# Modulation rows: from TensorE matmuls per block to VectorE products and one sum per row

## The chip, the cores and the metric

The program runs on one core of one Trainium2 chip. The metric is the device time of one execution in microseconds (us). Five engines run in parallel, each its own instructions in order: TensorE (PE), VectorE (DVE), ScalarE (ACT), GpSimd (POOL) and SyncE (SP), which here only issues DMAs. In the trace PEld is TensorE's weight load.

## The reference

Two models of two layers run one behind the other. The first (`first_block`, kernel layers F0 and F1) has a mixer of four branches and a SwiGLU feed-forward on 256 tokens of 1024 features. The second (`second_block`, kernel layers S0 and S1) takes its result `x` and a context `ctx` of another 256 tokens; its mixer has a gated branch, an attention and a convolution of 31 taps, and its feed-forward a convolution of 3 taps. Each layer of the second is modulated:

```python
cmod = adaln(c_ctx, w_mod[l], b_mod[l], 2 if last else 6)
sh1, sc1, g1, sh2, sc2, g2 = [m[:, None, :] for m in adaln(c, w_mod[l], b_mod[l], 6)]
hl = modulate(rms_norm_2(x_lat, norm1_g[l]), sh1, sc1)
...
x_lat = x_lat + g1 * mixer_merge(pa, o, pc, P, lam_init)
h2 = modulate(rms_norm_2(x_lat, norm2_g[l]), sh2, sc2)
x_lat = x_lat + g2 * conv_ffn(h2, P)
```

`adaln` is a product of the activated vector `c` (1024) with `w_mod[l]` (1024 x 6144) plus a bias. The kernel treats it as six rows for each of the two layers, twelve in all: row r of layer l is 1024 results, from a 1024 x 1024 part of `w_mod`. There are two vectors, one for `x` and one for the context; the last layer needs the context's rows 0 and 1 only.

## The kernel before

All matrix products go through split numbers: a weight unit of 128x1024 float32 (512 KB) is loaded by SP into `raw` (6 buffers), rounded to `hi` on ScalarE (L275), and the rest `lo = raw - hi` is formed on VectorE (L278); `hi` and `lo` have 4 buffers each. A product is then three matmuls, hi x hi, hi x lo and lo x hi (L509 to L511). Units are numbered through the kernel (`lo_405` is the split of unit 405), and all of F0, F1, S0, S1 read this one stream. F0 lies at about 0 to 600 us of the trace, F1 at 600 to 1255, S0 at 1260 to 1800, S1 from there to the end.

Beside the stream run "side lanes", work without matrix weights that is interleaved with the feed-forward of another layer. Beside F1's feed-forward (1012 to 1183 us) it is the context's mixer of S0, with the convolution's taps on VectorE (L1478, tile `cv`) and GpSimd (L1482). S0's feed-forward begins near 1447 us; its unit evaluates the short convolution and the gate on VectorE (L1526 to L1530, tiles `gh`, `th`), and `hl` is the split of its result.

The modulation rows are a generator (`mods`, L1116) that is advanced by `fill` from the gate and feed-forward loops of F0, F1 and S0. Each row has 8 blocks of 128x1024 (`wm`, 4 buffers, loaded by SP, L1137). A block costs four matmuls of 128x32 by 128x256 in full float32 (L1151, tile `am`), which sum over the 8 blocks in PSUM; the trace shows two records for each of these matmuls. Two blocks are done in a step (`MSTEP`). At the end of a row come a copy (`mo`, ScalarE), two transposes (L1161), the bias (L1164), and for rows 2 and 5 a DMA. In the layer's feed-forward of 512 tokens three steps follow each unit (`FF`).

The order of the instructions on each engine is not the order of the source: a scheduler that works with a timeline of its own moves the generator's instructions forward where it takes them to be ready.

## Time and profile before

| | us |
|---|---|
| median of three runs | 2175.38 (2171.88 to 2175.63) |
| the profiled execution | 2178.79 |
| its span, first to last instruction | 2176.7 |
| TensorE busy in it | 2109.6 (97%) |
| VectorE busy in it | 1413.5 (65%) |
| ScalarE busy in it | 1073.1 (49%) |
| GpSimd busy in it | 286.6 (13%) |

The profile is of one execution, with times from the span's start. The busy share says how much of the span an engine worked; the chain of work that ended last is followed back from the last instruction, and says which engine's work set the end, stage by stage. The mean granted clock of TensorE was 0.986 of full speed.

### The profile page before, as it was taken

How to read it: one execution, taken by the hardware profiler on the slowest of the kernel's cores; microseconds unless marked ns; L12 is line 12 of the kernel's file. 1: busy time of each engine (PE TensorE's matmuls, PEld its weight loads, DVE VectorE, ACT ScalarE, POOL GpSimd, SP SyncE). 2: the span in 40 equal slices, each digit the busy share in tenths (PEclk: the TensorE clock that was granted, in tenths of full speed). 3: DMA queues.
4: the chain of work that ended last, by engine and by line, in shares of the span. 5: the costliest groups of instructions: out<-in, count | busy, mean ns of one | idle time of the engine just before them, and what ended most of it. 6: DMA issues, size and time to landing. Idle time of an engine off the chain costs nothing.

```text
span 2176.7 us, 34980 instructions
## 1 busy us (share of the span) xinstructions
PE 2109.6 (97%) x13600; PEld 1818.3 (84%) x13600; DVE 1413.5 (65%) x2567; ACT 1073.1 (49%) x1900; POOL 286.6 (13%) x268
## 2 busy tenths in 40 slices
PE   8999999999999999999999997999999999899999
PEld 6788899889887888999889876687787888678997
DVE  7756656755579466668966479774435546976774
ACT  5555544634455556457554464653313335465552
POOL 2101112100032011121200035100000002610000
PEclk9999999999999999999999998899999999999999
DMA  9545655667765454556556654245535233224553
GB/s 334 162 139 175 204 188 191 228 151 260 240 185 178 134 161 145 159 181 223 194 115 203 212 206 145 95 145 186 197 112 192 88 90 114 88 87 141 185 189 116
DMA packets 102357, 366.71 MB, mean 168 GB/s; under 512 B 12560, under 2 KB 12720, under 8 KB 102192
## 3 DMA queue, kind: packets, MB, share of 16 engines
q1 hardware_dynamic: 99920, 358.65, 50.8%
q0 software_dynamic: 2272, 5.83, 1.0%
q8 instruction: 107, 1.75, 0.3%
q14 instruction: 58, 0.48, 0.1%
HBM read 361.76 MB, written 2.68 MB: 167 GB/s over the span
## 4 chain that ended last, share of the span: by engine, by line
PE 89%; DVE 6%; issue 2%; ACT 1%; DMA 1%; SPq 0%; POOL 0%; POOLq 0%; DVEq 0%; ACTq 0%
PE mm L509 26%; PE mm L510 26%; PE mm L511 26%; DVE cv L1478 2%; PE am L1151 2%; PE ax L1286 1%; DVE lo L278 1%; PE ax L936 1%; PE ax L1316 1%; ACT hi L275 1%; PE ay L591 1%; PE ay L462 1%; PE ax L891 1%; PE ax L889 1%; PE ax L1306 0%
## 5 line engine op out<-in xcount | busy, mean ns | idle before, releaser
L278 DVE TENSOR_TENSOR lo<-raw,hi 128x1024 fp32r<-128x1024 f32 (+2 forms) x552 | 697.0, 1265 | 527.8 <-ACT hi L275 494.0
L275 ACT ACTIVATE hi<-raw 128x1024 fp32r<-128x1024 f32 (+1 forms) x564 | 593.8, 1054 | 809.5 <-PE mm L510 384.6
L509 PE MATMUL mm<-hThi,hi 128*128 128x256 f32 (+1 forms) x2408 | 725.5, 303 | 6.7 <-DVE gu L1265 2.1
L510 PE MATMUL mm<-hTlo,hi 128*128 128x256 f32 (+1 forms) x2408 | 721.4, 300 | 4.8 <-issue 4.2
L511 PE MATMUL mm<-hThi,lo 128*128 128x256 f32 (+1 forms) x2408 | 719.3, 300 | 4.1 <-issue 3.5
L509 PEld LDWEIGHTS mm<-hThi,hi 128*128 128x128 f32 x2408 | 462.1, 193 | 45.4 <-issue 16.4
L510 PEld LDWEIGHTS mm<-hTlo,hi 128*128 128x128 f32 x2408 | 464.1, 193 | 21.6 <-issue 8.0
L511 PEld LDWEIGHTS mm<-hThi,lo 128*128 128x128 f32 x2408 | 462.9, 193 | 17.4 <-issue 2.8
L510 PE MATMUL mm<-lo,hThi 128*128 128x512 f32 (+2 forms) x480 | 183.5, 383 | 6.6 <-DVE lo L278 6.6
L509 PE MATMUL mm<-hi,hThi 128*128 128x512 f32 (+2 forms) x480 | 183.4, 388 | 5.2 <-DVE rb L580 3.1
L511 PE MATMUL mm<-hi,hTlo 128*128 128x512 f32 (+2 forms) x480 | 181.8, 381 | 0.5 <-DVE hTlo L472 0.5
L509 PE MATMUL mm<-hi,hh 128*128 128x512 f32 x440 | 171.5, 390 | 0.0
L510 PE MATMUL mm<-lo,hh 128*128 128x512 f32 x440 | 171.3, 389 | 0.0
L511 PE MATMUL mm<-hi,hl 128*128 128x512 f32 x440 | 170.9, 389 | 0.0
L509 PEld LDWEIGHTS mm<-hi,hThi 128*128 128x128 f32 x480 | 91.4, 191 | 26.6 <-issue 7.1
L510 PEld LDWEIGHTS mm<-lo,hThi 128*128 128x128 f32 x480 | 91.5, 191 | 26.3 <-DVE lo L278 8.4
L511 PEld LDWEIGHTS mm<-hi,hTlo 128*128 128x128 f32 x480 | 91.2, 190 | 17.3 <-issue 0.8
L509 PEld LDWEIGHTS mm<-hi,hh 128*128 128x128 f32 x440 | 82.6, 188 | 18.0 <-ACT hi L275 0.8
L511 PEld LDWEIGHTS mm<-hi,hl 128*128 128x128 f32 x440 | 82.6, 188 | 17.3
L510 PEld LDWEIGHTS mm<-lo,hh 128*128 128x128 f32 x440 | 82.6, 188 | 16.9
L1478 DVE SCALAR_TENSOR_TENSOR cv<-yp,kept,cv 128x256 f32<-128x256 f32 x120 | 86.1, 720 | 2.5 <-ACT cv L1474 0.7
L511 PE MATMUL mm<-yh,lo 128*128 128x256 f32 x256 | 72.8, 285 | 0.0
(348 smaller groups left out, 2757.4 us busy)
## 6 DMA issues: line engine op xcount, KB each, us to landing
raw<-in_w_f SPq DMA_DIRECT2D x364, 512.0 KB, 3.9
raw<-in_w_s SPq DMA_DIRECT2D x190, 512.0 KB, 3.5
wm<-in_w_mod SPq DMA_DIRECT2D x96, 512.0 KB, 5.1
bc<-csd POOLq DMA_DIRECT2D x32, 128.0 KB, 5.6
mrow<-md SPq DMA_DIRECT2D x6, 512.0 KB, 5.6
row<-in_rows SPq DMA_DIRECT2D x4, 512.0 KB, 5.8
raw<-in_w_f SPq DMA_DIRECT2D x4, 510.0 KB, 5.0
par<-in_par_s SPq DMA_DIRECT2D x2, 918.5 KB, 4.7
```

The source lines that it names most:

```text
L275: nc.scalar.activation(hi[:, :n], raw[:, :n], AF.Copy)
L278: ins = eng.tensor_sub(lo[:, :n], raw[:, :n], hi[:, :n].bitcast(F32)).ins
L462: nc.tensor.transpose(pss[k // 2][:, o:o + 128], xs[k // 4][:, 128 * (k % 4):128 * (k % 4) + 128], self.ident)
L509: nc.tensor.matmul(ps, ah, bh, start=first, stop=False)
L510: nc.tensor.matmul(ps, ah, bl, start=False, stop=False)
L511: nc.tensor.matmul(ps, al, bh, start=False, stop=last)
L591: nc.tensor.transpose(ps[:, b * 256 + t * 128:b * 256 + t * 128 + 128], nat[t][:, (b0 + b) * 128:(b0 + b) * 128 + 128], self.ident)
L889: nc.tensor.matmul(pair[j][:, 0:128], q[j][:, :128], k[j][:, :128], start=True, stop=True)
L891: nc.tensor.matmul(pair[j][:, 128:384], q[j][:, 128:], k[j], start=True, stop=True)
L936: nc.tensor.matmul(ps[64 * j:64 * j + 64, 0:256], vv, pt[:, 0:256], start=True, stop=False, skip_group_check=True)
L1151: nc.tensor.matmul(ps[32 * j:32 * j + 32, :256], self.ctp[:, 32 * kk:32 * kk + 32], loaded[i - k + kk][:, 256 * j:256 * j + 256], start=kk ...
L1478: nc.vector.scalar_tensor_tensor(c, y[:, j:j + 256], wj, c, op0=ALU.mult, op1=ALU.add)
```

## The change

Rows 0 and 1 of layer 0 stay as they are, but with one block in a step. For the ten other rows each block is multiplied on VectorE by its scalar per partition (`ct`, one column for each of the 8 blocks and the two vectors) and added up in SBUF: tile `macc`, 128x1024 float32, one for each vector, two instructions of 128x512 for each (L1169 of the new source for block 0, a plain product; L1171 for blocks 1 to 7, product and sum). After block 7 a matmul with a matrix of ones in one column (`onep`) sums over the partitions: 4 matmuls for each vector (L1177). In rows 2 to 5 of layer 1 only one vector is needed. The blocks have 2 buffers in place of 4, and `macc` has 2. The feed-forward of F0 and F1 advances the generator after three of four units, that of S0 by 2 steps for the first 64 and by 3 after that.

```diff
--- before.py
+++ after.py
@@ -27,7 +27,7 @@
 UNIT = 1024
 GROUP = {n: g for g, ns in (("a", "sm p pt dp at on yo osq"), ("c", "cth cv lj cn"), ("p", "tap"), ("g", "gz gsq gu ga"), ("m", "mo"))
          for n in ns.split()}
-KEEP = 1154 + 4 + 2 * (280 + 80 + 96 + 48)
+KEEP = 1154 + 4 + 64 + 2 * (280 + 80 + 96 + 48)
 LIM = 2.4e19
 OVER = 2.0 ** 118
 
@@ -310,7 +310,6 @@
     POOL_TAPS = 20
     HP = 300
     HELD = 3
-    FF = 3
     LOP = 4
     AHP = 0
     PACE = False
@@ -319,8 +318,8 @@
     FRONT = 7
     GHP = (300, 0)
     SIDE2 = 5
-    MSTEP = 2
-    WM = 4
+    MSTEP = 1
+    WM = 2
     HL = 4
     AHEAD = 4
     RA = 3
@@ -822,8 +821,10 @@
             fn(m, pg, pu, hi[:, o], lo[:, o])
             hid.append((hi[:, o], lo[:, o]))
             self.run_side(side)
-            if ntok == 512 or self.filled < 48:
-                self.fill(self.FF if ntok == 512 else 1)
+            if ntok == 512:
+                self.fill(2 if self.filled < 64 else 3)
+            elif i % 4 < 3 and self.filled < 48:
+                self.fill(1)
         return hid
 
     def swiglu_unit(self, m, pg, pu, hi, lo):
@@ -1123,6 +1124,10 @@
             nc.vector.scalar_tensor_tensor(th, th, 1.0, raw, op0=ALU.add, op1=ALU.mult)
             nc.vector.tensor_scalar(self.ct, th, 0.5, None, op0=ALU.mult)
             nc.gpsimd.memset(self.ctp, 0.0)
+            self.onep = self.keep(64)
+            nc.gpsimd.memset(self.onep, 0.0)
+            nc.gpsimd.memset(self.onep.rearrange("p (w m) -> p w m", m=32)[:, 0, 0:1], 1.0)
+            nc.gpsimd.memset(self.onep.rearrange("p (w m) -> p w m", m=32)[:, 1, 1:2], 1.0)
             nc.vector.tensor_copy(self.ctp.rearrange("p (k m) -> p k m", k=8)[:, :, 0:2], self.ct.rearrange("p (k w) -> p k w", k=8))
         bm = self.keep(48)
         nc.sync.dma_start(bm, dr["b_mod"][l])
@@ -1141,16 +1146,37 @@
             nw = 2 if l == 0 or r < 2 else 1
             while len(loaded) <= min(47, i + self.MSTEP):
                 load()
-            if k == 0:
+            early = l == 0 and r < 2
+            if k == 0 and early:
                 ps = self.ax_ps("am")
-            if (k + 1) % self.MSTEP:
-                yield
-                continue
-            for kk in range(k + 1 - self.MSTEP, k + 1):
-                for j in range(4):
-                    nc.tensor.matmul(ps[32 * j:32 * j + 32, :256], self.ctp[:, 32 * kk:32 * kk + 32],
-                                     loaded[i - k + kk][:, 256 * j:256 * j + 256], start=kk == 0, stop=kk == 7,
-                                     skip_group_check=True, tile_position=(0, 32 * j))
+            if early:
+                if (k + 1) % self.MSTEP:
+                    yield
+                    continue
+                for kk in range(k + 1 - self.MSTEP, k + 1):
+                    for j in range(4):
+                        nc.tensor.matmul(ps[32 * j:32 * j + 32, :256], self.ctp[:, 32 * kk:32 * kk + 32],
+                                         loaded[i - k + kk][:, 256 * j:256 * j + 256], start=kk == 0, stop=kk == 7,
+                                         skip_group_check=True, tile_position=(0, 32 * j))
+            else:
+                if k == 0:
+                    sums = [self.wp.tile([128, UNIT], F32, tag="macc", name=f"macc{l}_{r}_{w}", bufs=2) for w in range(nw)]
+                for h in range(2):
+                    o = slice(512 * h, 512 * h + 512)
+                    for w in range(nw):
+                        c = self.ct[:, 2 * k + w:2 * k + w + 1]
+                        if k == 0:
+                            nc.vector.tensor_scalar(sums[w][:, o], loaded[i][:, o], c, None, op0=ALU.mult)
+                        else:
+                            nc.vector.scalar_tensor_tensor(sums[w][:, o], loaded[i][:, o], c, sums[w][:, o],
+                                                           op0=ALU.mult, op1=ALU.add)
+                if k == 7:
+                    ps = self.ax_ps("am")
+                    for w in range(nw):
+                        for j in range(4):
+                            nc.tensor.matmul(ps[32 * j:32 * j + 32, :256], self.onep[:, 32 * w:32 * w + 32],
+                                             sums[w][:, 256 * j:256 * j + 256], start=w == 0, stop=w == nw - 1,
+                                             skip_group_check=True, tile_position=(0, 32 * j))
             if k < 7:
                 yield
                 continue
```

Three places show how the instructions lie now. `lo_n` is unit n's split, `macc{l}_{r}_{w}` the sum of row r of layer l for vector w, `wm{l}_{r}_{k}` block k. The first is VectorE in F1's feed-forward (about 1015 us), before:

```order
L1220 TENSOR_TENSOR kept_77<-kept_77 128x64
L1225 TENSOR_TENSOR kept_77<-kept_77 128x2x16 x2
L278 TENSOR_TENSOR lo_296_11123<-raw_296_11047,hi_296_11122 128x1024
L278 TENSOR_TENSOR lo_297_11160<-raw_297_11065,hi_297_11159 128x1024
L1461 SCALAR_TENSOR_TENSOR yp_1137_11150<-cth_1138_11151,mm_1135_11088 128x256
L278 TENSOR_TENSOR lo_298_11191<-raw_298_11089,hi_298_11190 128x1024
L278 TENSOR_TENSOR lo_299_11229<-raw_299_11120,hi_299_11228 128x1024
L1461 SCALAR_TENSOR_TENSOR yp_1142_11218<-cth_1143_11219,mm_1140_11156 128x256
L1478 SCALAR_TENSOR_TENSOR cv_1139_11155<-yp_1137_11150,kept_77,cv_1139_11155 128x256 x3
```

and now:

```order
L278 TENSOR_TENSOR lo_296_11115<-raw_296_11039,hi_296_11114 128x1024
L1251 TENSOR_TENSOR kept_77<-kept_77 128x2x16
L1171 SCALAR_TENSOR_TENSOR macc0_4_0_6246<-wm0_4_2_11570,kept_77,macc0_4_0_6246 128x512
L1171 SCALAR_TENSOR_TENSOR macc0_4_1_6247<-wm0_4_2_11570,kept_77,macc0_4_1_6247 128x512
L1487 SCALAR_TENSOR_TENSOR yp_1136_11142<-cth_1137_11143,mm_1134_11080 128x256
L278 TENSOR_TENSOR lo_297_11152<-raw_297_11057,hi_297_11151 128x1024
L1171 SCALAR_TENSOR_TENSOR macc0_4_0_6246<-wm0_4_2_11570,kept_77,macc0_4_0_6246 128x512
L1171 SCALAR_TENSOR_TENSOR macc0_4_1_6247<-wm0_4_2_11570,kept_77,macc0_4_1_6247 128x512
```

Between the splits of units 296 and 297 and behind 297 stand products of row 4 of layer 0, and no longer only the splits and the side work.

The second is TensorE in S0's feed-forward (about 1475 us), before, behind the matmuls of unit 409, with the semaphores that an instruction waits for:

```order
L510 MATMUL mm_1733_15905<-hTlo_1655_15227,hi_409_15815 128x512
L511 MATMUL mm_1733_15905<-hThi_1654_15226,lo_409_15816 128x512
L1151 MATMUL am_1731_15903<-wm1_1_1_15885,kept_77 32x256 x2
L1151 MATMUL am_1731_15903<-wm1_1_2_15901,kept_77 32x256 [waits DMAHW1_49]
L1151 MATMUL am_1731_15903<-wm1_1_2_15901,kept_77 32x256 x3
L1151 MATMUL am_1731_15903<-wm1_1_3_15976,kept_77 32x256 [waits DMAHW4_49]
L1151 MATMUL am_1731_15903<-wm1_1_3_15976,kept_77 32x256 x3
L509 MATMUL mm_1738_16000<-hThi_1648_15220,hi_410_15845 128x512 [waits Activation_49]
```

and now, behind those of unit 408:

```order
L509 MATMUL mm_1728_15925<-hTlo_1655_15270,hi_408_15789 128x512
L510 MATMUL mm_1728_15925<-hThi_1654_15269,lo_408_15790 128x512
L1177 MATMUL am_1732_16009<-macc1_0_0_15762,kept_77 32x256 [waits DVE_49]
L1177 MATMUL am_1732_16009<-macc1_0_0_15762,kept_77 32x256
L508 MATMUL mm_1729_15926<-hThi_1648_15263,hi_409_15845 128x512 [waits Activation_49]
L509 MATMUL mm_1729_15926<-hTlo_1649_15264,hi_409_15845 128x512
L510 MATMUL mm_1729_15926<-hThi_1648_15263,lo_409_15846 128x512
```

The blocks' matmuls, which waited for DMAs, are gone, and the first sum of row 0 of layer 1 stands there and waits for VectorE.

The third is VectorE at the end of that row, before, around the split of unit 411:

```order
L1527 SCALAR_TENSOR_TENSOR gh_1727_15873<-mm_1725_15811,kept_77,gh_1727_15873 128x2x255
L1529 SCALAR_TENSOR_TENSOR th_1728_15874<-th_1728_15874,gh_1727_15873 128x512
L1530 TENSOR_TENSOR th_1728_15874<-th_1728_15874,mm_1726_15812 128x512
L278 TENSOR_TENSOR lo_411_15909<-raw_411_15747,hi_411_15908 128x1024
L840 TENSOR_TENSOR hl_1724_15810<-th_1728_15874,hh_1723_15809 128x512
L278 TENSOR_TENSOR lo_412_15939<-raw_412_15813,hi_412_15938 128x1024
L1526 SCALAR_TENSOR_TENSOR gh_1734_15966<-mm_1732_15904,kept_77,gh_1734_15966 128x2x255
```

and now:

```order
L1555 SCALAR_TENSOR_TENSOR th_1721_15818<-th_1721_15818,gh_1720_15817 128x512
L1171 SCALAR_TENSOR_TENSOR macc1_0_0_15762<-wm1_0_6_15919,kept_77,macc1_0_0_15762 128x512
L1552 SCALAR_TENSOR_TENSOR gh_1726_15903<-mm_1724_15841,kept_77,gh_1726_15903 128x2x255
L1171 SCALAR_TENSOR_TENSOR macc1_0_1_15763<-wm1_0_6_15919,kept_77,macc1_0_1_15763 128x512
L1171 SCALAR_TENSOR_TENSOR macc1_0_0_15762<-wm1_0_7_15997,kept_77,macc1_0_0_15762 128x512
L1171 SCALAR_TENSOR_TENSOR macc1_0_1_15763<-wm1_0_7_15997,kept_77,macc1_0_1_15763 128x512
L278 TENSOR_TENSOR lo_411_15930<-raw_411_15787,hi_411_15929 128x1024
L1556 TENSOR_TENSOR th_1721_15818<-th_1721_15818,mm_1719_15774 128x512
L1171 SCALAR_TENSOR_TENSOR macc1_0_0_15762<-wm1_0_7_15997,kept_77,macc1_0_0_15762 128x512
```

Products of blocks 6 and 7 stand among the instructions of the gate, and two of the gate's (L1556 and L1553) stand behind the split of unit 411.

## Rows read from the trace of the kernel before

**Rows 1.** Page, busy time of each engine; then the chain that ended last, by engine.

```profile
PE 2109.6 (97%) x13600; PEld 1818.3 (84%) x13600; DVE 1413.5 (65%) x2567; ACT 1073.1 (49%) x1900; POOL 286.6 (13%) x268
PE 89%; DVE 6%; issue 2%; ACT 1%; DMA 1%; SPq 0%; POOL 0%; POOLq 0%; DVEq 0%; ACTq 0%
```

**Rows 2.** Busy time of each engine in three stretches; window, its length, busy per engine (instructions).

```profile
core 0: us, PE busy (x) PEld busy (x) DVE busy (x) ACT busy (x) POOL busy (x), PEclk, DMA share, GB/s
420.00:558.00 138.00, 133.24 (x1127) 127.67 (x1126) 77.01 (x111) 59.10 (x88) 3.47 (x3) 0.96 0.69 209
1012.00:1154.00 142.00, 133.14 (x1058) 123.67 (x1058) 110.93 (x238) 80.64 (x187) 27.21 (x31) 0.96 0.59 181
1447.00:1471.00 24.00, 24.00 (x131) 19.94 (x130) 19.12 (x45) 11.80 (x16) 0.00 (x0) 1.00 0.46 154
```

**Rows 3.** Pieces of the chain, in order of time: start, us, what (x records).

```profile
406.24 0.56 PE am L1151 x6
556.12 1.00 PE am L1151 x16
...
1270.07 4.55 DMA wm<-in_w_mod
...
1456.73 0.99 PE am L1151 x12
1479.69 1.42 PE am L1151 x20
...
1517.97 1.00 PE am L1151 x16
1530.12 1.86 PE am L1151 x32
...
1692.32 1.86 PE am L1151 x32
```

**Rows 4.** The chain by line, in 1012 to 1154, 1260 to 1320, 1447 to 1525.

```profile
by line: PE mm L509 21.4%; PE mm L510 20.7%; PE mm L511 20.5%; DVE cv L1478 7.5%; issue 5.8%; DVE lo L278 5.0%; PE ax L1286 4.5%; PE ax L1316 3.5%; ACT hi L275 1.4%; PE am L1151 1.4%; PE ax L1306 1.2%; DVE rc L1297 0.9%; DVE mx L1292 0.8%;
by line: PE mm L510 20.3%; PE mm L509 18.8%; PE mm L511 18.5%; DVE cv L1478 11.9%; DMA wm<-in_w_mod 7.6%; DVE lo L278 6.7%; issue 5.1%; PE am L1151 4.8%; DVE rb L580 2.3%; DVE ss L1242 2.0%; DVE ss L415 1.2%; DVE ra L569 1.1%; DVEq L278 0.0
by line: PE mm L509 31.2%; PE mm L510 30.4%; PE mm L511 29.8%; PE am L1151 8.2%; PE am L1161 0.6%
```

**Rows 5.** Timeline of VectorE, single rows: start, us, line, operation, out<-in, shapes.

```profile
1034.40 0.94 DVE L1478 SCALAR_TENSOR_TENSOR cv<-yp,kept,cv 128x256 f32<-128x256 f32 x1
1035.27 0.41 DVE L1265 SCALAR_TENSOR_TENSOR gz<-gsq,mm 128x256 f32<-128x256 f32 x1
...
1446.38 1.21 DVE L278 TENSOR_TENSOR lo<-raw,hi 128x1024 fp32r<-128x1024 f32 x1
...
1451.44 0.74 DVE L1526 SCALAR_TENSOR_TENSOR gh<-mm,kept,gh 128x510 f32<-128x510 f32 x1
1452.10 1.22 DVE L278 TENSOR_TENSOR lo<-raw,hi 128x1024 fp32r<-128x1024 f32 x1
...
1469.72 1.22 DVE L278 TENSOR_TENSOR lo<-raw,hi 128x1024 fp32r<-128x1024 f32 x1 [0.18 <-ACT hi L275]
```

**Rows 6.** Instructions of one line on VectorE: duration in ns, min/median/max.

```profile
L618 DVE SCALAR_TENSOR_TENSOR x<-yg,rs,x x3: 745/751/1783, 1259.5 to 1260.9; 128x512 f32<-128x512 f32 x3
...
L1478 DVE SCALAR_TENSOR_TENSOR cv<-yp,kept,cv x120: 461/485/2630, 1025.6 to 1897.9; 128x256 f32<-128x256 f32 x120
```

**Rows 7.** Timeline of TensorE, two rows; in brackets the idle time before, and its releaser.

```profile
1274.66 0.64 PE L1151 MATMUL am<-wm,kept 128*32 128x256 f32 x8 [1.43 <-DMA wm<-in_w_mod]
...
1474.09 0.39 PE L509 MATMUL mm<-hThi,hi 128*128 128x512 f32 x1
```

**Rows 8.** DMA issues of the modulation blocks: KB each, median us to landing.

```profile
wm<-in_w_mod SPq DMA_DIRECT2D x96, 512.0 KB, 5.1
```

**Rows 9.** Timeline of GpSimd, the taps of the convolution, 20 in a row.

```profile
1028.10 20.09 POOL L1482 TENSOR_TENSOR cv<-cv,tap 128x256 f32<-128x256 f32 x20 [10.93 <-ACT tap L1481]
```

**Rows 10.** Groups by line, VectorE: busy us, mean ns of one, then idle before.

```profile
L1478 DVE SCALAR_TENSOR_TENSOR cv<-yp,kept,cv 128x256 f32<-128x256 f32 x120 | 86.1, 720 | 2.5 <-ACT cv L1474 0.7
```

## The prediction

> **What bounds the kernel now.** I read the page's busy times and its chain first. TensorE is busy in 97% of the span and VectorE in 65%; 89% of the chain that ended last is TensorE's own work and 6% VectorE's [rows 1]. So an instruction taken from TensorE shortens the kernel, and one given to VectorE is free, only where VectorE has room. An average does not say where that is, so I went to the stages, and in each asked for three things: the chain's share of the modulation matmuls, the busy time of VectorE, and what ends TensorE's waits.
>
> There are four stages. In F0's feed-forward (420 to 558 us) VectorE works 77.0 of 138 us [rows 2], and all eight modulation bursts from 406 to 556 us are pieces of the chain [rows 3]: room, and something to win. In F1's feed-forward (1012 to 1154 us), where the context stream's convolution taps run as side work, VectorE works 110.9 of 142 us [rows 2], and the chain runs through VectorE's taps for 7.5% and its splits for 5.0%, through the modulation matmuls for 1.4% [rows 4]: hardly any room, and hardly anything to win. At the start of S0 (1260 to 1320 us) the chain has 4.8% of modulation matmuls and 7.6% of waiting for a modulation block, but 11.9% of VectorE's taps behind them [rows 4]. In S0's feed-forward (1447 us on) the chain is TensorE alone [rows 4], with 17 bursts in it between 1456 and 1692 us [rows 3].
>
> **What goes.** Ten of twelve rows leave TensorE: 80 of 96 blocks with 4 matmuls each, 320 of 384. What returns is one sum per row: 6 rows of 8 matmuls and 4 rows of 4, 64. The net is 256 fewer. A burst of 8 matmuls (two records each, x16) holds the chain for 1.00 us, one of 16 for 1.86 us [rows 3], so about 0.12 us for one. All 256 are worth at most 256 x 0.12 = 31 us, if nothing takes their place.
>
> **What comes.** 256 VectorE instructions of 128x512: 224 multiply-adds and 32 plain products. The nearest row is the kernel's own multiply-add of that size with a scalar per partition, in the feed-forward convolution: 0.74 us, and the next instruction begins 0.66 us after it began (1451.44 to 1452.10) [rows 5]. That one reads PSUM and SBUF. The one with both tensors in SBUF, as here, has 751 ns as its median, but 1783 ns at worst [rows 6]. I take a pitch of 0.67 us for each, from the median; the upper end comes with the rivals. Sum: 256 x 0.67 = 172 us of VectorE, on top of 1413.5. It must be hidden entirely, and the new order does not spread it evenly: 60 of the instructions stand in each of F0's and F1's feed-forward stretches, and all 128 of layer 1 in S0's.
>
> **F0.** 60 x 0.67 = 40 us more on 77.0 makes 117 of 138 us. It fits. Eight bursts go, the first of 0.56 and seven of 1.00 us (the last of them stands in [rows 3]), 7.6 us; two row sums of 1.00 come back. **-5.6 us.**
>
> **F1.** 60 x 0.67 = 40 more on 110.9 makes 151 in a stretch of 142 us. VectorE would be over by 9 us, if all of its own work stayed in it and none of its waits closed up. The new order puts 28 of these instructions between the splits lo_296 and lo_304, ahead of the taps that stood there (shown above). The splits are produced several units ahead of their use, so part of the 9 us is absorbed. Ends: -2.0 (1.4% of 142, nothing lost) and +9. I take the half nearer to the full stretch, **+4 us**.
>
> **Start of S0.** The modulation matmuls and the wait for their block (4.55 us in the chain [rows 3], 1.43 of TensorE's own idle time [rows 7]) leave this place, as layer 1's first product is now placed at lo_405. 12.4% of 60 is 7.4 us; but behind them VectorE's taps are in the chain, and they will be late next. Between 0 and -7.4 I take **-4 us**.
>
> **S0's feed-forward, the first row.** Here a new wait arises. The sum of row 0 stands on TensorE right behind the matmuls with lo_408, and its operand is finished on VectorE just before lo_411 (both shown above). TensorE executes in order, so the whole stream waits behind it. When is VectorE there? Before, lo_405 starts at 1446.4 and lo_411 at 1469.7 [rows 5]; between them VectorE has about 18.5 us of work (19.1 in 1447 to 1471, less lo_411's part [rows 2]), of which two instructions of the gate, 2 x 0.67, now stand later. 27 new instructions stand between: 27 x 0.67 = 18. So VectorE is there at 1446.4 + 17 + 18 = 1481.5. TensorE is there at 1474.1, where it begins with unit 409 before [rows 7], less one burst of 1.0: 1473.1. **The stall is 8 us.** Ends: 5, if more of VectorE's work is put off, and 12, if each new product waits for its block besides (below). Up to 1518 us six bursts go, one of 1.42 and five of 1.00 (0.99 the first) [rows 3], 6.4 us; one sum of 1.0 comes. Together +8 + 1.0 - 6.4 = **+2.6 us**.
>
> **S0's feed-forward, the rest.** Now VectorE is a row ahead of its reader: the sum of row 2 stands behind unit 423 on TensorE, its operand is ready before lo_424, and a split is made more than two units before its use (lo_411 at 1469.7 [rows 5], when TensorE has yet to begin with unit 409 [rows 7]). Eleven bursts go, from 1530 to 1692 us: 1.86 for the first and the last [rows 3]; with the nine between, 224 records in all at 1.00/16, 14.0 us. One sum of 8 matmuls and four of 4 come back, 3.0. **-11.0 us.**
>
> **The loads.** Count, size and queue of the 96 loads stay. But the blocks have two buffers in place of four, and a buffer is now released by VectorE. In row 0 of layer 1 four multiply-adds, some three instructions of the gate of like size and every other time a split (1.22 us [rows 5]) lie between a release and the need of the block that takes its place: 7 x 0.67 = 4.7, or 5.9 us; a block takes 5.1 us from issue to landing [rows 8]. I price it at nothing, since VectorE's own lateness covers the difference, and keep the other end as a rival. Behind a waiting load SP holds back the loads of weights, whose six buffers cover tens of us in S0.
>
> **Sum.** -5.6 + 4 - 4 + 2.6 - 11.0 = -14.0 us, against the profiled execution of 2178.8: 2164.8. That execution lies 3.4 above the median of the three runs, so against 2175.4 the forecast is **2161 us**.
>
> **Rival A: all is hidden.** VectorE runs far enough ahead that no sum waits. F0 -5.6, F1 -2.0, start -7.4, S0 -6.4 + 1.0 - 11.0 = -16.4: -31.4, and 2144 us against the median. For it: VectorE's 65%. Against it: the 142-us stretch, and the place of row 0's sum.
>
> **Rival B: the two buffers.** If the load is 1 us late for each block after the first two of rows 0 and 1 of layer 1, VectorE, which is the later engine there, is held 14 x 1 = 14 us, and TensorE with it: -14.0 + 14, that is 2175 us, no change. For it: TensorE already waited 1.43 us for a block with four buffers [rows 7]. Against it: 4.7 to 5.9 us against 5.1 leaves as much room for no wait at all.
>
> **Rival C, the slower side: the products in F1 cost more than their median.** GpSimd's taps run beside them: 20 from 1028 to 1048 us [rows 9]. In the same microseconds VectorE's tap multiply-add with both tensors in SBUF takes 0.94 us [rows 5], where its median is 485 ns [rows 6], while the multiply-add beside it that reads PSUM takes 0.41 [rows 5]. Over the kernel the taps have a mean of 720 ns [rows 10], 1.48 times the median. By that factor each of the 60 products of F1 costs 0.35 us more: +21 us, in the one stretch where VectorE is full. The sum becomes -14.0 + 21 = +7, 2182 us. It decides from 14/60 = 0.23 us per product on; below that the kernel is still faster. Against it: GpSimd's 20 taps last 20.09 us [rows 9] of the stretch's 142, and the taps on VectorE, which pay the same now, are only put off.
>
> The Trainium skill speaks against this change here (page "SBUF — State Buffer", section "Who interferes with whom"): a VectorE instruction with two SBUF inputs contends with a GpSimd instruction that reads SBUF, and whichever comes second is blocked until the other ends; one with a single SBUF input is not. The trace agrees: 0.94 and 0.41 us side by side [rows 5]. By that rule VectorE can be held no longer than GpSimd itself is busy, 20 us at most in this stretch, of which the taps of now pay a part already; rival C's 21 us would then be its upper end, and not its middle.
>
> **How the numbers follow.** Forecast 0.46; A 0.15; B 0.17; C 0.22. The kernel is called changed beyond 0.2%, 4.4 us, about what a measurement can tell. Faster: all of the forecast and A, and a bit of B: 0.64. Same: most of B and the lower end of C: 0.13. Slower: the rest, 0.23. The range has to reach A's lower end (start and F0 a little better than priced) and C's: 2139 to 2186. The forecast's own range is 2150 to 2170.
>
> **What will show it.** Right: TensorE idle for some 8 us about 1475 us, ended by VectorE's line of the products; no gain in F1; from 1530 us on the stream of matmuls unbroken but for row sums. The products' median near 0.74 us, with a mean above it in F1 alone. Rival A: that idle time is absent and S0's start is early by over 5 us. Rival B: VectorE idle before products, ended by the DMA of a block, some 14 times about 1 us. Rival C: F1's stretch longer than 142 us by over 15 us, with products of 1 us and more beside GpSimd's taps. I am wrong altogether if VectorE's lateness reaches PSUM: if TensorE waits for gate results in every unit of S0's feed-forward, not once.

## The result, and the profile after

| | before | changed |
|---|---|---|
| median, us (six runs each) | 2175.83 (2171.88 to 2180.49) | 2153.59 (2149.02 to 2158.38) |
| ratio | | 0.989 (95%: 0.9868 to 0.9912) |
| profiled execution, us | 2178.79 | 2158.38 |
| its span, us | 2176.7 | 2156.2 |

The changed kernel is faster by 22.2 us; 14.0 were forecast. The direction and the range held, the size was 8 us short. Below it turns out that the 14 had several errors in it which partly cancelled, and that both kernels carry a cost of 14 to 16 us that the prediction never named.

The first view is the page of the changed kernel: busy time of each engine, then the chain that ended last by engine, then by line. The code's lines have shifted: products are L1169 (first block) and L1171, row sums L1177, the matmuls per block that are left L1158, the weight stream L508 to L510.

```profile
PE 2071.8 (96%) x13088; PEld 1801.9 (84%) x13088; DVE 1557.3 (72%) x2823; ACT 1070.1 (50%) x1900; POOL 293.8 (14%) x271
PE 84%; DVE 9%; DMA 3%; issue 2%; ACT 1%; POOL 0%; SPq 0%; POOLq 0%; DVEq 0%; ACTq 0%
PE mm L508 25%; PE mm L510 25%; PE mm L509 25%; DMA wm<-in_w_mod 2%; DVE cv L1504 2%; DVE lo L278 2%; DVE macc L1171 2%; PE ax L1312 1%; PE ax L937 1%; PE ax L1342 1%; ACT hi L275 1%; PE am L1158 1%; PE ay L461 1%; PE ay L590 1%; PE ax L892 1%
```

Against [rows 1]: TensorE has lost 512 records, two for each of the 256 net matmuls, and 37.8 us of busy time; VectorE has gained 143.8 us. TensorE's share of the chain falls from 89 to 84%, and the loads of modulation blocks (`wm<-in_w_mod`) and the products now hold 2% each (to one more digit 2.5% and 1.8%, 54 and 39 us). The gain of about 38 us on TensorE has thus been paid back in part through VectorE and through DMAs.

The next view answers [rows 2], the same three stretches with the busy time of each engine.

```profile
core 0: us, PE busy (x) PEld busy (x) DVE busy (x) ACT busy (x) POOL busy (x), PEclk, DMA share, GB/s
420.00:558.00 138.00, 133.46 (x1049) 128.34 (x1049) 112.17 (x173) 60.31 (x92) 4.93 (x5) 0.98 0.79 239
1012.00:1154.00 142.00, 129.27 (x1043) 122.73 (x1043) 137.49 (x259) 75.11 (x163) 28.53 (x26) 0.95 0.64 206
1447.00:1471.00 24.00, 17.52 (x77) 12.70 (x76) 23.36 (x36) 9.08 (x13) 0.00 (x0) 0.86 0.56 169
```

VectorE in F0's feed-forward is at 112 of 138 us (117 expected), and in F1's at 137.5 of 142. In the third stretch TensorE has lost 6.48 us, and that is one single wait, on TensorE's timeline (start, duration, instruction, idle time before it and what ended it):

```profile
1451.53 0.39 PE L510 MATMUL mm<-hThi,lo 128*128 128x512 f32 x1
1458.40 1.07 PE L1177 MATMUL am<-macc,kept 128*32 128x256 f32 x4 [6.48 <-DVE macc L1171]
1459.40 0.80 PE L508 MATMUL mm<-hThi,hi 128*128 128x512 f32 x1
```

This is the stall that was forecast at 8 us: the sum of layer 1's row 0, at its place behind the matmuls of unit 408, waiting for VectorE.

**Where the time went, stage by stage.** Both kernels read the same numbered weight units, so the start of the first matmul that reads unit n (the trace's matmuls, numbered by the program's order) is a clock that both share. The table has that time in the changed kernel minus that time in the one before, as the difference over each stage (negative is a gain). The last column is the same for a second pair of kernels, e2 and e1 below, in which one disturbance is out of the way; it is given here so that the table stands once.

| stage (units) | forecast | changed - before | e1 - e2 |
|---|---|---|---|
| start and F0's mixer (to 114) | 0 | -5.8 | -6.1 |
| F0's feed-forward (114 to 162) | -5.6 | -5.9 | -4.1 |
| F1's mixer (162 to 294) | 0 | -1.7 | -3.0 |
| F1's feed-forward (294 to 366) | +4.0 | -1.3 | +7.2 |
| start and mixer of S0 (366 to 408) | -4.0 | -7.6 | -2.6 |
| S0's feed-forward, first six units (408 to 414) | +2.6 to unit 416, then -11.0 | +6.8 | +6.8 |
| S0's feed-forward, the rest (414 to 456) | | -2.8 | -13.7 |
| after that (456 to 558) | 0 | -2.2 | -1.6 |
| sum | -14.0 | -20.5 | -17.1 |

-20.5 is also the difference of the two spans. How well does this clock repeat? Between e1 and e9, two executions of one kernel on two chips, it differs by 1.1 us up to unit 12, by 1.5 us in F1's mixer, and by at most 0.6 us in every other stage.

Four stages differ much from the forecast: the start, F1's feed-forward, S0's start, and S0's feed-forward behind its first row. The waits of VectorE say where to look. The view is that of the tile `macc` in the changed kernel: durations of the products in ns (min/median/max), then VectorE's idle time ahead of them (us, times).

```profile
L1171 DVE SCALAR_TENSOR_TENSOR macc<-wm,kept,macc x224: 727/745/1225, 413.3 to 1612.1; 128x512 f32<-128x512 f32 x112
...
  DMA wm<-in_w_mod: 32.2, 14
```

VectorE waited 14 times for a block, 32.2 us in all. The number of times is rival B's, but the size is not uniform. Two of the waits hold 20.8 us, as VectorE's timeline shows (the last row ahead of each wait, and the wait):

```profile
482.78 0.42 DVE L841 TENSOR_TENSOR hl<-tt,hh 128x256 fp32r<-128x256 f32 x1
493.41 1.42 DVE L1171 SCALAR_TENSOR_TENSOR macc<-wm,kept,macc 128x512 f32<-128x512 f32 x2 [10.21 <-DMA wm<-in_w_mod]
...
1557.51 1.42 DVE L1171 SCALAR_TENSOR_TENSOR macc<-wm,kept,macc 128x512 f32<-128x512 f32 x2 [1.35 <-DMA wm<-in_w_mod]
1569.53 1.41 DVE L1171 SCALAR_TENSOR_TENSOR macc<-wm,kept,macc 128x512 f32<-128x512 f32 x2 [10.61 <-DMA wm<-in_w_mod]
```

A block takes 4.4 us from issue to landing at the median of this kernel (5.1 before, [rows 8]); here one is in the chain with 18.15 us from 475.16 and one with 13.26 us from 1556.18. What the DMAs did at the first place, in windows of 10 us of the changed kernel (the last two columns are the DMA share and GB/s):

```profile
480.00:490.00 10.00, 10.00 (x85) 10.00 (x84) 3.20 (x6) 3.91 (x6) 0.00 (x0) 1.00 0.54 37
490.00:500.00 10.00, 5.46 (x31) 5.26 (x30) 6.59 (x10) 2.69 (x4) 0.00 (x0) 0.67 0.91 341
```

For 10 us the DMA engines are busy in 54% of the time and move 37 GB/s; then they move 341. TensorE runs on its reserve of splits and stands idle for 4.5 us after 490. The mean granted clock of that window is 0.67, and of 495 to 500 us it is 0.50, the lower of its two levels (1.2 of 2.4 GHz), so the idle time is followed by slow matmuls. The chain has one of the same shape ahead of the hole and one behind it:

```profile
467.87 0.12 PE mm L510
...
497.03 0.21 PE mm L510
```

What was issued just ahead of each hole is on GpSimd's timeline:

```profile
469.85 1.81 POOL L1195 DMA_DIRECT2D md<-kept  x2 [35.73 <-DVE kept L1190]
...
1553.41 0.96 POOL L1195 DMA_DIRECT2D md<-kept  x1 [136.85 <-DVE kept L1190]
```

These are the stores of the gate rows 2 and 5, which are in both kernels: 1024 floats of one vector go from `col` (128 partitions x 8) to DRAM in a transposed order, so that by the access pattern no two neighbours of a partition lie side by side in DRAM and each run is a single float of 4 bytes. (The trace does not show these runs: it records such a store as 16 packets of 256 bytes for each vector.) The kernel before has the same hole behind the same store (issued at 460.24 and at 1122.99), in its own windows:

```profile
465.00:480.00 15.00, 10.24 (x85) 8.96 (x84) 4.29 (x7) 4.03 (x6) 0.00 (x0) 0.85 0.46 26
1125.00:1145.00 20.00, 15.77 (x119) 15.35 (x119) 6.85 (x10) 6.34 (x12) 0.00 (x0) 0.91 0.53 28
```

In its chain they are two pieces called "issue", of 3.54 us at 473.75 and 4.23 us at 1137.70, which I had read past. That these stores cause the holes was a theory at this point; the first pair of experiments is on it.

### The profile page after: what moved, and what is told of

It reads as the page before. It is cut to its first block, busy times and chain, and to the rows that moved or that the text cites. A ratio compares the mean times of both kernels' runs of the same rounds, so it can differ in the third digit from the quotient of the medians.

```text
span 2156.2 us, 34229 instructions
## 1 busy us (share of the span) xinstructions
PE 2071.8 (96%) x13088; PEld 1801.9 (84%) x13088; DVE 1557.3 (72%) x2823; ACT 1070.1 (50%) x1900; POOL 293.8 (14%) x271
## 4 chain that ended last, share of the span: by engine, by line
PE 84%; DVE 9%; DMA 3%; issue 2%; ACT 1%; POOL 0%; SPq 0%; POOLq 0%; DVEq 0%; ACTq 0%
PE mm L508 25%; PE mm L510 25%; PE mm L509 25%; DMA wm<-in_w_mod 2%; DVE cv L1504 2%; DVE lo L278 2%; DVE macc L1171 2%; PE ax L1312 1%; PE ax L937 1%; PE ax L1342 1%; ACT hi L275 1%; PE am L1158 1%; PE ay L461 1%; PE ay L590 1%; PE ax L892 1%
## 5 line engine op out<-in xcount | busy, mean ns | idle before, releaser
L508 PE MATMUL mm<-hThi,hi 128*128 128x256 f32 (+1 forms) x2408 | 723.1, 302 | 14.6 <-DVE gz L1291 12.1
L510 PE MATMUL mm<-hThi,lo 128*128 128x256 f32 (+1 forms) x2408 | 717.2, 299 | 4.6 <-DVE lo L278 4.5
L508 PEld LDWEIGHTS mm<-hThi,hi 128*128 128x128 f32 x2408 | 460.2, 192 | 44.6 <-issue 13.6
L510 PEld LDWEIGHTS mm<-hThi,lo 128*128 128x128 f32 x2408 | 461.0, 192 | 24.2 <-DVE lo L278 5.0
L508 PE MATMUL mm<-hi,hThi 128*128 128x512 f32 (+2 forms) x480 | 181.7, 386 | 5.2 <-DVE rb L579 3.1
L1171 DVE SCALAR_TENSOR_TENSOR macc<-wm,kept,macc 128x512 f32<-128x512 f32 x224 | 161.8, 763 | 31.5 <-DMA wm<-in_w_mod 31.3
L510 PE MATMUL mm<-hi,hTlo 128*128 128x512 f32 (+2 forms) x480 | 180.2, 378 | 0.0
L508 PE MATMUL mm<-hi,hh 128*128 128x512 f32 x440 | 173.1, 394 | 4.2 <-DVE xn L1564 4.2
L510 PE MATMUL mm<-hi,hl 128*128 128x512 f32 x440 | 172.6, 393 | 0.0
L509 PEld LDWEIGHTS mm<-lo,hThi 128*128 128x128 f32 x480 | 90.9, 190 | 28.3 <-DVE lo L278 12.4
L508 PEld LDWEIGHTS mm<-hi,hThi 128*128 128x128 f32 x480 | 90.9, 190 | 26.4 <-issue 6.9
L510 PEld LDWEIGHTS mm<-hi,hTlo 128*128 128x128 f32 x480 | 90.5, 189 | 16.3 <-issue 0.3
L508 PEld LDWEIGHTS mm<-hi,hh 128*128 128x128 f32 x440 | 83.6, 190 | 22.4 <-issue 5.0
L510 PEld LDWEIGHTS mm<-hi,hl 128*128 128x128 f32 x440 | 83.7, 190 | 17.7
```

The source lines that it names most:

```text
L508: nc.tensor.matmul(ps, ah, bh, start=first, stop=False)
L509: nc.tensor.matmul(ps, ah, bl, start=False, stop=False)
L510: nc.tensor.matmul(ps, al, bh, start=False, stop=last)
L1171: nc.vector.scalar_tensor_tensor(sums[w][:, o], loaded[i][:, o], c, sums[w][:, o], op0=ALU.mult, op1=ALU.add)
```

## The experiments

**The gate rows stored in runs (e1, e2).** The same edit in both kernels: `col` is transposed on TensorE, copied by ScalarE, and stored as 8 runs of 512 bytes per vector. Nothing else changes.

```diff
-            for which in range(nw):
-                if r in (2, 5):
-                    nc.gpsimd.dma_start(md[which, r // 3, :].rearrange("(j p) -> p j", p=128), col[:, which, :])
+            if r in (2, 5):
+                ps = self.ax_ps("am")
+                nc.tensor.transpose(ps[:8 * nw, :128], col[:, :nw, :].rearrange("p w m -> p (w m)"), self.ident)
+                mr = self.tmp("mo", 256)
+                nc.scalar.activation(mr[:8 * nw, :128], ps[:8 * nw, :128], AF.Copy)
+                for which in range(nw):
+                    nc.gpsimd.dma_start(md[which, r // 3, :].rearrange("(j p) -> j p", p=128), mr[8 * which:8 * which + 8, :128])
```

The changed kernel with it:

> Edit: in the changed kernel the gate rows (r = 2 and 5) go to DRAM as 8 runs of 512 bytes per vector (one transpose on TensorE and one copy on ScalarE more per row) and not as 1024 single floats; results are the same. Theory 1: the single-float stores leave the DMA queues almost empty-handed for 10 to 15 us (trace of the changed kernel: 39 GB/s at 485 to 490 us, 29 GB/s at 1560 to 1565 us), and VectorE, which executes in order, stands behind a product that waits for its block (10.2 us at 493 us, 10.6 us at 1569 us). Then the time falls by 8 to 16 us against the changed kernel, to 2138 to 2146 us, and VectorE's idle time before products that wait for a block falls from 32 us to under 12. Theory 2: VectorE is simply full in these stretches and the store only coincides: within 3 us of 2154.

Measured: 2139.64 us (2132.13 to 2142.38), 0.9826 of before (0.9799 to 0.9853). The kernel before with it:

> Edit: the same store by runs of 512 bytes in the kernel before. Theory 1 (the single-float store starves the weight loads): TensorE's unexplained gaps of 3.5 us at 474 us and 4.2 us at 1138 us go, and the time falls by 6 to 10 us, to 2166 to 2170 us; less than in the changed kernel, where VectorE stands behind two buffers. Theory 2: the gaps have another cause, and the time stays within 3 us of 2176.

Measured: 2159.20 us (2156.87 to 2165.57), 0.9926 of before (0.9901 to 0.9952): 16.4 us less, where I expected 6 to 10. So six stores of 4 KB cost the changed kernel 14 us and the one before 16 (by medians; the interval of e2 alone reaches from 10 to 22). In e1's windows, the two that showed the hole:

```profile
480.00:490.00 10.00, 10.00 (x86) 10.00 (x85) 9.98 (x17) 5.33 (x8) 0.00 (x0) 1.00 0.80 259
490.00:500.00 10.00, 10.00 (x85) 10.00 (x84) 9.62 (x14) 4.18 (x7) 0.00 (x0) 1.00 0.84 284
```

The hole is gone: 259 GB/s in place of 37, TensorE unbroken at full clock. The store itself, in the list of DMA issues (queue, KB each, median us from issue to landing), of the changed kernel:

```profile
md<-kept POOLq DMA_DIRECT2D x6, 4.0 KB, 12.5
```

and of e1:

```profile
md<-mo POOLq DMA_DIRECT2D x6, 4.0 KB, 3.4
```

VectorE's waits for blocks fall from 32.2 to 15.8 us in e1, in 15 pieces, all in S0 and none over 2.1 us. Shown: the holes come from the stores. The trace's records of single packets agree: a load's packet of 4096 bytes lasts 159 ns at the median, but up to 6511 ns between 465 and 495 us of the changed kernel, and up to 1174 ns between 474 and 495 us of e1.

By the shared clock e1 gains 6.6 us on the changed kernel in F0's feed-forward (units 138 to 144), and 10.7 in S0's (426 to 438); e2 gains on before 8.2 at 126 to 138, 7.3 at 324 to 330 and 6.6 between 366 and 408, most of it at 384 to 396, where a read-back of the gate row (`mrow<-md`) stood in its chain. (These add up to 22 us, since the two profiled executions lie 21.9 us apart and the medians 16.4.) Of the 6.6 us in F0's feed-forward 4.5 are the idle time shown above; the rest fits the slow matmuls behind it: by estimate some 4 us of them, at 0.21 us in place of 0.12, lose 2. So the stores hit the two kernels at different places, and the pair e2 and e1 is the better measure of the change itself: 2139.64 against 2159.20, 19.6 us.

The Trainium skill says (page "DMA: Bandwidth & Descriptors", section "Issuing engines are not separate DMA queues") that DMAs run on the same 16 DMA engines and interleave, whichever engine initiated them. The trace agrees: a store issued by GpSimd held up blocks that SP loads, 18.15 us against 4.4 at the median.

**Four blocks and four raw buffers (e4).** If two buffers make VectorE late, four should not; SBUF takes them only if `raw` gives up two.

```diff
-    RAW = 6
+    RAW = 4
...
-    WM = 2
+    WM = 4
```

> Edit: in the changed kernel the modulation blocks have four buffers as before, and the weight stream four in place of six, which frees the memory. Theory 1: products that wait for their block (32 us of VectorE's idle time in all) are what S0's feed-forward loses; with four buffers that falls below 12 us and the time falls by 6 to 13 us, to 2141 to 2148 us. Rival: the weight stream then has no cover for late loads itself, splits wait for raw units, and the time stays at 2154 us or rises.

Measured: 2156.44 us (2154.0 to 2158.43), 0.9906 (0.988 to 0.9931): no different from the changed kernel. The tile `macc` of e4, VectorE's waits ahead of products:

```profile
  DMA wm<-in_w_mod: 6.6, 3
```

The block waits fall from 32.2 us to 6.6, and the 13.1 us that the changed kernel lost at units 426 to 438 of S0 become 1.2, though the store of single floats is still there (TensorE busy throughout 1550 to 1590 us). So in S0 the store and the two buffers lose those microseconds together: with the store alone (e4) 1.2 us are lost there, with the two buffers alone (e1) 2.4. But with four `raw` buffers the kernel is 7 us later at unit 12 (made up again by unit 114) and loses 9 us at units 343 to 348, where the weight stream now runs dry: ScalarE waits up to 14.5 us there for a raw unit. The stall at the first sum is untouched, 6.57 us. That it isn't the blocks which make that sum late is thereby shown.

**Two blocks in the kernel before (e8).** The same two settings as in the change, and nothing else of it.

```diff
-    MSTEP = 2
-    WM = 4
+    MSTEP = 1
+    WM = 2
```

> Edit: the kernel before, with one block in a step and two buffers for blocks (MSTEP 1, WM 2), and nothing else of the change. The changed kernel is 4.4 us ahead at unit 12, 52 us into the span, which the forecast did not have. Theory 1: fewer blocks are loaded ahead of the first weights; then this kernel has the same lead of 4 to 5 us at unit 12. Whether it keeps it is open: with two buffers the blocks of ten more rows wait on TensorE, which may cost more than 4 us: 2171 to 2180 us. Theory 2: the lead at unit 12 comes from the order of the matmuls: no lead there.

Measured: 2205.65 us (2198.09 to 2212.34), 1.012 (1.0088 to 1.0152): 25 us slower, far outside the 2171 to 2180 of theory 1. Two things follow. At unit 12 it is 4.5 us early, as the changed kernel is (4.4): the gain at the start comes from these two settings alone (which of the two is not shown). SP's first loads were two modulation blocks at 10.24 us and two more at 16.22 before; now one at 9.88 and one at 13.38, so the first weights come earlier. And behind unit 108 it loses everything again. TensorE's waits for blocks (us in all, times, the longest), the longest of them on its timeline, and the windows of 10 us ahead of that:

```profile
PE am L1151 <- DMA wm<-in_w_mod: 20.3, 4, 9.4
...
493.34 1.08 PE L1151 MATMUL am<-wm,kept 128*32 128x256 f32 x8 [9.39 <-DMA wm<-in_w_mod]
...
480.00:490.00 10.00, 3.95 (x33) 3.75 (x32) 4.02 (x7) 2.69 (x4) 0.00 (x0) 0.95 0.58 32
```

With the rows on TensorE the two settings cost some 30 us (4.5 early, then 25 late), and the store of single floats has its share in that: it was issued at 469.16, and the longest wait stands behind its hole of 32 GB/s. With ten rows on VectorE the changed kernel lives with two buffers, and e1, where the stores don't disturb it, loses 2.4 us against e2 at units 426 to 438. I read that as a matter of who waits: before, the stream of matmuls itself stood behind a late block. These two runs do not show it, since e8 has the disturbing stores and e1 has not; e7 below is the fairer comparison.

**Row 4 back on TensorE (e3).** To measure what the products cost F1, one row of F1 goes back.

```diff
-            early = l == 0 and r < 2
+            early = l == 0 and (r < 2 or r == 4)
```

> Edit: in the changed kernel row 4 of layer 0, whose products stand in F1's feed-forward, stays on TensorE like rows 0 and 1 (24 matmuls more, 32 VectorE instructions of 128x512 fewer). Theory 1: these products delay the splits at 1000 to 1033 us, where the kernel loses 12.6 us of its lead within six units; without them the lead of 13 us is kept there, TensorE pays 24 x 0.12 = 3 us, and the time falls by 5 to 10 us, to 2144 to 2149 us. Theory 2: the lead lost there is regained behind, since TensorE has slack until 1140 us (the lead is back at 11 us by then): 2154 to 2158 us.

Measured: 2169.05 us (2166.58 to 2174.61), 0.9961 (0.9943 to 0.998), 15 slower than the changed kernel. This run does not tell the theories apart: the scheduler put the products of row 5 at units 295 to 303, just where row 4's had been, with the same loss of 13.6 us there (12.6 in the changed kernel), TensorE had to wait for one of row 4's blocks (3.05 us; +6 between units 180 and 183), and row 5's store, issued at 1177.10, made its hole where TensorE then stood for 3.79 and 1.97 us (+8 between 342 and 348).

**Rows 4 and 5 of layer 0 elsewhere (e5, e6).** On top of e1, both rows go from F1's feed-forward into its gate loop, where VectorE is 42% busy (12.53 of 30 us, 700 to 730 us of e9, a repetition of e1). e6 also spreads the products in S0 more thinly.

```diff
-                if l == 0 and m % 2:
+                if m % 2 and self.filled < 48:
```

> Edit: the changed kernel with the store by runs of 512 bytes, and the generator advanced in F1's gate loop too (up to 48 steps), so that the products of rows 4 and 5 of layer 0 stand at units 184 to 215 and none in F1's feed-forward. Theory 1: products in the stretch where VectorE is full cost F1 7 us net of what TensorE saves; then unit 300 keeps its lead (loss under 3 us, before 12.6), and the time falls by 5 to 8 us against 2139.6, to 2131 to 2135 us. Theory 2: F1 loses its lead for another reason, or the gate loop pays the same: 2138 us or more.

Measured: 2157.05 us (2155.62 to 2160.29), 0.99 (0.9874 to 0.9926), so 17 slower than e1, not faster. And yet the question is answered: the loss at unit 300 vanishes (the shared clock stands at +8.1 against the kernel before at units 294 and 300 alike, where e1 goes from -21.5 to -8.9), and F1's feed-forward as a whole comes out 10 us better than in e1. The products cost that stage about 10 us. But the gate loop loses 27 us from unit 192 to 216 (from -19.6 to +7.3 against the kernel before). Its windows, and the waits on TensorE's timeline:

```profile
710.00:720.00 10.00, 3.33 (x19) 0.85 (x18) 10.00 (x24) 1.19 (x2) 0.00 (x0) 0.69 0.86 302
720.00:730.00 10.00, 4.71 (x18) 3.05 (x20) 6.79 (x39) 0.51 (x2) 1.55 (x3) 0.50 0.12 45
...
716.57 1.07 PE L1177 MATMUL am<-macc,kept 128*32 128x256 f32 x4 [6.22 <-DVE macc L1171]
726.36 1.01 PE L992 MATMUL ax<-kept 128*16 128x256 f32 x2 [4.72 <-DVE kept L986]
```

VectorE is full from 700 to 720 us, first the sum waits for it, then F1's short serial chain of small VectorE instructions (L986), which before ran in VectorE's gaps. The granted clock falls to 0.50 behind that, the lower level (1.2 of 2.4 GHz). A mean of 42% was no room, either.

e6, against the kernel of e5:

```diff
-                self.fill(2 if self.filled < 64 else 3)
+                self.fill(1 if self.filled < 56 else 3)
```

> Edit: as e5_rows45_in_gates, and in S0's feed-forward one step per unit for the first eight and three after that; row 0 of layer 1 keeps its place, rows 1 to 5 stand 7 to 16 units later. Theory 1: in S0 only the wait for row 0's sum costs (6.5 us), the density of the later products does not, once the store is out of the way: within 2 us of e5. Theory 2: the density of the products at units 413 to 436 costs too: 3 to 7 us below e5.

Measured: 2158.06 us (2156.61 to 2158.4), 0.9901 (0.9881 to 0.9921), the same as e5.

**Layer 1 on TensorE (e7).** e1 with layer 1's six rows as before, but with two buffers.

```diff
-            early = l == 0 and r < 2
+            early = l == 1 or r < 2
```

> Edit: the changed kernel with the store by runs, but all rows of layer 1 stay on TensorE as in the kernel before; products only for rows 2 to 5 of layer 0. The forecast's terms for layer 1 are -4 at the start of S0 and -8.4 in its feed-forward. If they hold, the time rises by 8 to 13 us against 2139.6, to 2148 to 2153 us. If layer 1's products bring nothing (the wait for the sum eats them), it stays at 2138 to 2143 us.

Measured: 2164.81 us (2162.82 to 2168.13), 0.9935 (0.9912 to 0.9958), 25 slower than e1; I had expected 8 to 13. Between units 366 and 456 it falls behind e1 by 16.4 us, and at 336 to 342 it loses 10.5 where e1 loses 2.8; TensorE's idle time for blocks is 7.8 us, in 3 waits. With two buffers, then, layer 1's products on VectorE are worth 16.4 us there. e2 helps to divide them: it has the same rows on TensorE with four buffers, and is 9.5 us behind e1 in these units (2.6 - 6.8 + 13.7, from the table). So by estimate 9.5 are the matmuls themselves, against the 12.4 that the forecast had for these stages, and 7 the two settings.

**Where the first sum stands (e9, e10, e11).** e9 is the kernel of e1 once more, as the measure on the same chip. e10 is e9 with the edit of e6. e11 lets F1's feed-forward run seven units before row 5's products.

> The kernel of e1 (the changed kernel with the store by runs) once more, as the reference of e10 and e11 on the same chip: 2136 to 2143 us.

Measured: 2142.26 us (2135.19 to 2143.11), 0.9824 (0.9803 to 0.9846).

> Edit: the kernel of e1, and in S0's feed-forward one step per unit for the first eight, three after that: rows 1 to 5 of layer 1 stand 7 to 16 units later on VectorE, row 0 keeps its place. Theory 1: after row 0's sum nothing in S0 waits for products, so their density is free: within 2 us of e9. Theory 2: the density costs at units 413 to 436 (in the profiles of e5 and e6 4.5 us lie between the two there, though their medians agree): 3 to 6 us below e9.

Measured: 2144.25 us (2141.32 to 2145.86), 0.9839 (0.9821 to 0.9858), the same as e9: the pace of the generator's steps in S0 decides nothing.

```diff
-            elif i % 4 < 3 and self.filled < 48:
+            elif self.filled < 48 and (i >= 7 if self.filled >= 33 else i % 4 < 3):
```

> Edit: the kernel of e1, with F1's feed-forward steps from its eighth unit on and one per unit; row 5's products of layer 0 stand at units 330 to 343 in place of 320 to 330, row 4 keeps its place at 295 to 303. Theory 1: of F1's 7 us most belongs to row 4 (lost by unit 300, of which some 8 come back by 306), and row 5 costs the rest, at units 330 to 342: later, in a stretch where VectorE has more room, it costs less, and the time falls by 2 to 5 us below e9. Theory 2: row 5 costs the same wherever it stands: within 2 us.

Measured: 2140.10 us (2134.45 to 2141.75), 0.9819 (0.9798 to 0.984): 2 us under e9, which the scatter does not resolve. But its order has the first sum of row 0 one unit later, behind unit 409, and TensorE's timeline there reads

```profile
1451.93 0.63 PE L1177 MATMUL am<-macc,kept 128*32 128x256 f32 x4 [1.64 <-DVE macc L1171]
1455.04 1.29 PE L1177 MATMUL am<-macc,kept 128*32 128x256 f32 x12 [1.13 <-DVE macc L1171]
```

1.64 and 1.13 us in place of 6.5 (e9: 6.47), and units 408 to 414 lose 1.4 us, not 6.8. e5, whose order also has that sum behind unit 409, waits 1.64 and 1.14 us and loses the same 1.4. The wait is a matter of the place in the order: one unit later, and 3.7 us of it are gone. F1's feed-forward, for which e11 was meant, gains 1 us on e9 as a whole: row 5 later costs about the same. e9 and e11 are also the best kernels of the study, some 38 to 40 us below the one before.

## Why the prediction was right in direction and 8 us short

**Right: F0's feed-forward.** -5.6 forecast, -5.9 measured (-4.1 in the clean pair). VectorE had the room that [rows 2] promised.

**Right: the stall at row 0's sum.** 8 us forecast, from two orders and VectorE's timeline; 6.48 measured, at the very instruction. That it comes from the place and not from the blocks is confirmed by e4 (four buffers, 6.57) and by e11 and e5 (one unit later). Nowhere else in S0 did a sum wait so long, as forecast.

**Right in kind: F1.** No gain was to be had there. In the clean pair the stage is 7.2 us worse, inside the ends -2 and +9 and above the +4 taken, and e5 prices the products there at 10. The chain by line from 1000 to 1030 us of the changed kernel begins:

```profile
by line: DVE macc L1171 39.7%; DVE lo L278 26.1%; issue 10.2%; DVE hTlo L471 7.8%; DVE mx L1318 4.7%; DVE cv L1504 2.9%; DVE kept L1251 2.6%; DVE yp L1487 2.2%; DVE rc L1323 2.0%; DVE kept L1246 1.4%; DVE gsq L1289 1.1%; DVEq L278 0.4%; DVE
```

Where TensorE's matmuls led in [rows 4], the chain is VectorE's, product and split by turns. That the raw comparison shows -1.3 is luck: the kernel before lost 7.3 us there to its own store at 1122.99, and the changed kernel's falls where it costs nothing.

**Wrong: "The loads. ... I price it at nothing", and with it the -11.0 of S0's rest.** Measured -2.8. The step that failed is the sentence that VectorE's lateness covers the difference between 4.7 or 5.9 us of reach and 5.1 us of landing. It failed in two ways. First, that reach was worked out for row 0, with four products to a block, and taken for all rows. For rows 0 and 1 it holds, no product of theirs waited for a block. Rows 2 to 5 of layer 1 need one vector and have two products to a block, and 13 of the 14 waits lie in its rows 3 to 5 (the products counted in the program's order). Twelve of the fourteen are about 1 us (32.2 less 20.8, over 12), and such waits cost little: with the stores out of the way 15 of them remain in rows 2 to 5, yet the rest of S0 gains 13.7, more than forecast, and the whole feed-forward of S0 -6.9 against -8.4. Second, nothing covers a landing behind a store of single floats on the other queue: 13 us stop VectorE, in whose order splits and gate stand behind the product, and with it TensorE.

**Missed: the start, -4.4 by unit 12.** I priced the smaller `MSTEP` and `WM` in S0 alone and did not go through SP's first loads. e8 shows the cause.

**Missed: "issue" in the chain.** It had 5.8% of F1's stretch [rows 4], and I did not ask what lay behind it. The piece of 4.23 us there is the store's hole: e2 gains 7.3 us at that place. S0's start is -7.6 in place of -4 for the same reason: the read-back of the gate row stood in the chain of the kernel before; the clean pair has -2.6.

**How much was luck.** By the table S0's feed-forward came out 12.4 us worse than forecast, and all the other stages together 18.9 better, so 6.5 of the difference is left in the spans. The total is nearer to its forecast than these parts are. (The 28 products of F1 that the prediction puts between lo_296 and lo_304 begin four earlier, just ahead of lo_296; its argument does not hang on that.)

**The rivals.** A (all hidden, 2144) fell with the stall at 1458.40. B had the right resource and, by chance, the right count, 14 waits, and the wrong place: none in rows 0 and 1, short ones in rows 3 to 5, and two long waits behind stores, one of them in F0. C needed 0.23 us more per product of F1. The next rows are the products in two windows of the changed kernel, 995 to 1060 us and 1060 to 1260 us (busy us, mean ns of one, idle before):

```profile
L1171 DVE SCALAR_TENSOR_TENSOR macc<-wm,kept,macc 128x512 f32<-128x512 f32 x28 | 23.8, 891 | 0.0
...
L1171 DVE SCALAR_TENSOR_TENSOR macc<-wm,kept,macc 128x512 f32<-128x512 f32 x28 | 19.6, 741 | 0.0
```

In the first, 20 taps of GpSimd run for 24.38 us from 1019.26; beside the second row's products, which lie at 1098 to 1139 us, GpSimd is idle. The mean goes from 741 to 891 ns, 0.15 us for half of the products and nothing for the other half: 4 us, not 21. The timelines are sharper than the mean. Two products that begin just before the taps take 1.40 us together, four in the midst of the taps 4.61:

```profile
1018.36 1.40 DVE L1171 SCALAR_TENSOR_TENSOR macc<-wm,kept,macc 128x512 f32<-128x512 f32 x2
1019.26 24.38 POOL L1508 TENSOR_TENSOR cv<-cv,tap 128x256 f32<-128x256 f32 x20 [15.15 <-ACT tap L1507]
1023.39 4.61 DVE L1171 SCALAR_TENSOR_TENSOR macc<-wm,kept,macc 128x512 f32<-128x512 f32 x4
```

Nine products, which begin between 1023 and 1040 us, take 1.13 to 1.23 us each, the other 19 of the 28 take 0.74. So rival C's price for one product was too low, and its number of products that pay, 60, far too high.

The Trainium skill's rule (page "SBUF — State Buffer", section "Who interferes with whom"), that a VectorE instruction with two SBUF inputs contends with a GpSimd instruction that reads SBUF, agrees with these rows, and so does the bound drawn from it, that GpSimd's own busy time limits the damage. The taps paid too: 24.38 us for 20, where [rows 9] had 20.09.

**What stays open.** F1's mixer gained 1.7 (3.0 in the clean pair), of which up to 1.5 can be scatter, and I have traced no cause. Nor is the 10 us that e5 shows for F1 split between VectorE's fullness, the 4 us of slower products, and TensorE's clock, which the forecast left out: over 1012 to 1154 us the granted clock is 0.95 in e1 and 0.99 in e2.

## What to carry to other kernels

Before moving work to an engine with room, go through the stages for two things, not one: how full that engine is, and what stands behind the moved instruction in its order if its operand is late once by 10 us; buffers chosen for the median landing are no cover for that. Give the reduced result a place in the bound engine's order one unit later than looks necessary: here one unit took away 3.7 of 6.5 us of waiting, though the time of the whole kernel moved by less than its scatter. And follow every "issue" of several microseconds in the chain down to the DMA windows of that time: 16 us of a tuned kernel lay behind six stores of 4 KB.

## What the runs showed of the hardware

A store of 1024 single floats per vector (by its access pattern), two vectors issued together, brought the whole core's DMAs to 26 to 37 GB/s for 10 to 20 us, at a DMA share near one half; issue to landing was 12.5 us (median). As 8 runs of 512 bytes the same data landed in 3.4 us and left no mark on the throughput (259 GB/s in the same microseconds). The store of one vector alone, in S0, made a shorter hole of the same depth. In the kernel before, where it was issued at 1537.69, TensorE worked through it:

```profile
1540.00:1550.00 10.00, 10.00 (x56) 7.58 (x55) 4.63 (x7) 2.35 (x4) 0.00 (x0) 1.00 0.32 32
```

A weight unit lasts 5.8 us there by the shared clock (units 414 to 456) and 3.2 us in F0's feed-forward, so the same buffers reach further; that this is why it cost nothing is argued, not shown. I had not expected six stores of 4 KB to cost 14 to 16 us, as much as the forecast gave the whole change.

The product with both inputs in SBUF (128x512, float32, scalar per partition) takes 745 ns at the median, the same as the multiply-add of nearly that size (128x510) that reads PSUM (0.74 us, [rows 5]), and without GpSimd's taps beside it, it keeps to that: a mean of 741 to 747 ns in all stretches but the one.
